# Transposing eight of twelve row blocks by DMA instead of on TensorE, and moving up the last value block's work in the paired feed-forward parts

## The chip, the cores and the metric

The kernel runs on one core of a Trainium2 chip. A core has five engines that run side by side, each through its own list of instructions in order: TensorE (PE) multiplies matrices and can transpose a 128x128 tile by multiplying it with an identity, VectorE (DVE) and ScalarE (ACT) work on tiles in on-chip memory, GpSimd (POOL) and SyncE (SP) here mostly issue transfers (DMAs). Semaphores make one engine wait for another. The metric is device time in microseconds (us) of one execution; the kernel before takes 1997.59 us, the median of three runs (1996.73 to 1998.44).

## The reference

One decoder layer for 256 tokens with 2048 features, all in 32-bit floats:

```python
hn = rmsnorm(h, norm_mix_w)
q, k, v, g_ret, xr, yr, g_a, g_b = jnp.split(hn @ w_in, offsets, axis=-1)
ret_out = silu(g_ret) * head_groupnorm(chunkwise_retention(rotary(q), rotary(k), v))
rnn_out = gelu(yr) * rg_lru(causal_dwconv(xr), ...)
merged = sigmoid(g_a) * (ret_out @ w_proj_ret) + sigmoid(g_b) * (rnn_out @ w_proj_rnn)
h = h + merged @ w_mix_out
h = h + memory_cross_attention(rmsnorm(h), rmsnorm(mem), xa_w_q, xa_w_k, xa_w_v, xa_w_o)
up = causal_dwconv(rmsnorm(h) @ ffn_w_up)          # 2 x 5632 columns: gate, value
gate, val = jnp.split(up, 2, axis=-1)
h = h + (silu(gate) * val) @ ffn_w_down
out = rmsnorm(h, final_norm_w)
```

The sigmoid is written with a tanh, so `merged` is formed at twice its value and has to be scaled by 0.5.

## The kernel before

**How a product is made.** The weights come as tiles of 4 x 128 rows by 512 columns (1 MB, `raw`). ACT rounds a tile to the format that TensorE multiplies at full speed (`hi`, line 286), DVE subtracts to get what was lost (`lo`, line 287). The activations are split in the same way into two halves of one tile (`s`, lines 552 to 557 and 578, 579). A product needs three matmuls: high part of the activation with `hi` (line 362), low part with `hi` (363), both called uppers here, and high part with `lo` (369), the lowers. Four k steps by two row halves make a unit of 24 matmuls for one weight tile.

**Units and pairs.** `gemm_n` computes one block of 512 output columns in four units, one per weight tile. `pair_out` and `pair_add` (both through `pair_products`) compute two neighbouring blocks in eleven units with fewer multiplications, as in Strassen's scheme. Units p0 to p3 take rows of the activations; q1 to q7 take pieces of them or sums of pieces (`ss`, made by `sums`, lines 501 to 510), and need sums of weight tiles: DVE adds two held tiles after q5 (line 294, tile A plus B) and after q6 (line 292, tile A plus C), and a POOL DMA adds a tile from memory into a held one (line 267). A held tile can be changed only once `hi` and `lo` are made from it.

**Order of work.** `units` steps through the plan of all units. Before a unit's matmuls it prepares weight tiles up to two units ahead (`prefetch`). `later(n, fn)` puts a function off until n more units have passed; small steps (transposes, splits, reloads) are placed so between the units. The framework schedules what the code emits once, when the kernel is built, and fixes the order on each engine; `tc.high_priority(URGENT)` moves work ahead of other work that is ready. There are six buffers for `raw` and three for `hi` and `lo`. SP issues weight loads, row loads and stores, and transposing DMAs, in order.

**Turning rows.** A product leaves its result with tokens as rows; the next product needs features as rows. In three places PE turns them: `transposed` (line 532) does four 128x128 transposes into one piece of 256 features; each block of 512 columns has two pieces. `turn_merged` turns the four blocks of `merged` during w_proj_rnn; `turn` and `turn_rows` turn the residual rows `hrow` after w_mix_out and after xa_w_o: twelve blocks in all, 24 groups of four transposes, 96 transposes. The residual of w_mix_out is made as a pair of blocks 0 and 1, then blocks 2 and 3 singly; that of xa_w_o as two pairs.

In other places DMAs turn the rows: `row_planes` copies the 32-bit words of a block into two planes of 16-bit halves (ACT, two copies, line 757), `turn_planes` transposes them with two DMAs on SP (line 1205 before), and `join_planes` puts one piece together again (ACT, two copies, line 763). So the feed-forward's up product (`up`) and the attention's keys work.

**Beside it.** In `residual`, `squares` sums the squares of each finished block for the norm (ACT, line 1113). During w_mix_out, `memory_rows` also loads a block of the memory's rows (line 208) and sums its squares. The residual is stored for later (`hkept`, line 1139).

**Feed-forward.** It runs in parts of 4, 4 and 3 blocks. In a part of four the down product works in pairs. Each up block is turned by DMA, scaled (line 1271), convolved (`conv`: ACT line 1281, DVE line 1283), and gated (`hidden`: lines 1354 to 1356, 555, 556). For the last value block of a paired part, the two joins are put off by 2 and 4 units into the down product's first pair.

Of the kernel before, what the change touches and what calls it, by code (L numbers as in the profile page):

```python
# [9 lines left out]
F32 = mybir.dt.float32  # L10
F32R = mybir.dt.float32r
I32 = mybir.dt.int32
U16 = mybir.dt.uint16
AF = mybir.ActivationFunctionType
ALU = mybir.AluOpType
AX = mybir.AxisListType

P = 128
D = 2048
S = 256  # L20
# [6 lines left out]
FF = 5632  # L27
# [127 lines left out]
def hybrid_layer(  # L155
# [34 lines left out]
    def big(shape, dt=F32, s="b"):  # L190
        return bp.tile(shape, dt, tag="big", name=nm(s))

    def tmp(s="t"):
        return tp.tile([P, 2, S], F32, tag="tmp", name=nm(s))
# [109 lines left out]
    def later(n, fn):  # L304

        pending.append((step[0] + n + 1, fn))
# [187 lines left out]
    def sums(src, scale=None):  # L494

        t = big([P, 2, BW], F32R, s="ss")
        m = tmp("sm")
        f = m.rearrange("p a n -> p (a n)")
        s1, s2, s3, s4 = (f[:, i * P : (i + 1) * P] for i in range(4))
        a11, a21, a12, a22 = (src[:, j, i * P : (i + 1) * P] for j in range(2) for i in range(2))  # L500
        dve.tensor_tensor(out=s1, in0=a21, in1=a22, op=ALU.subtract)
        dve.tensor_tensor(out=s2, in0=s1, in1=a11, op=ALU.subtract)
        dve.tensor_tensor(out=s3, in0=a11, in1=a21, op=ALU.subtract)
        dve.tensor_tensor(out=s4, in0=a12, in1=s2, op=ALU.add)
        if scale is None:
            act.copy(t[:, 0, :], f)
            dve.tensor_tensor(out=t[:, 1, :], in0=f, in1=t[:, 0, :].bitcast(F32), op=ALU.subtract)
        else:
            act.mul(t[:, 0, :], f, scale)
            dve.scalar_tensor_tensor(  # L510
                out=t[:, 1, :], in0=f, scalar=scale, in1=t[:, 0, :].bitcast(F32), op0=ALU.mult, op1=ALU.subtract
            )
        return t
# [34 lines left out]
    def split_pair(src, scale=None):  # L548

        t = big([P, 2, BW], F32R, s="s")  # L550
        if scale is None:
            act.copy(t[:, :, 0:S], src)
            dve.tensor_tensor(out=t[:, :, S:BW], in0=src, in1=t[:, :, 0:S].bitcast(F32), op=ALU.subtract)
        else:
            act.mul(t[:, :, 0:S], src, scale)
            dve.scalar_tensor_tensor(  # L556
                out=t[:, :, S:BW], in0=src, scalar=scale, in1=t[:, :, 0:S].bitcast(F32),
                op0=ALU.mult, op1=ALU.subtract,
            )
        return t  # L560
# [13 lines left out]
    def split_cols(src, wcol):  # L574

        t = big([P, 2, BW], F32R, s="s")
        for j in range(2):
            act.activation(t[:, j, 0:S], src[:, j, :], AF.Identity, scale=wcol(j))
            dve.scalar_tensor_tensor(
                out=t[:, j, S:BW], in0=src[:, j, :], scalar=wcol(j), in1=t[:, j, 0:S].bitcast(F32),  # L580
                op0=ALU.mult, op1=ALU.subtract,
            )
        return t
# [170 lines left out]
    def planes(t, rows, cs=slice(0, BW)):  # L754

        for i in range(2):
            act.copy(t[:, :, i, cs], words(rows)[:, :, :, 1 - i])

    def join_planes(d, pr):

        t = tmp("jp")
        for i in range(2):
            ins = act.copy(words(t)[:, :, :, 1 - i], d[:, i, 2 * pr : 2 * pr + 2, :])  # L763
            if i == 0:
                tc.keep_in_program_order(ins)
        return t

    class KeptRows(list):
        def __init__(self, name, wcol=None):
            self.rows = dp.tile([4, S, 2 * BW], U16, name=name)  # L770
# [244 lines left out]

    def turn_merged(m, pr):
        for t in transposed(m[:, :, pr * S : (pr + 1) * S]):
            if len(merged) < KC:
                c = tmp("mt")
                act.mul(c, t, 0.5)  # L1020
                merged.append(split_pair(c))
                merged_sums.append(sums(c))
            else:
                merged.append(split_pair(t, 0.5))

    for b in range(4):
        recurrent(b)
# [36 lines left out]
    for b in range(4):  # L1064
        m = sig[4 + b]
        gated(m, gemm_n("w_proj_rnn", 0, rnn, NT, b * BW))
        dve.tensor_add(m, m, sig[b])
        for pr in range(2):
            later(pr, lambda m=m, pr=pr: turn_merged(m, pr))


    hrow = [load_rows(x, c) for c in range(2)]
# [2 lines left out]
    def residual(w, st, ssum, out, osum, wcol, steps=None):  # L1075

        ss = sp_.tile([P, 2, 4], F32, tag="ss0", name=nm("ss"))
        for bs in RESIDUAL[w]:
            if steps:
                steps(bs[0])  # L1080
            if len(bs) > 1:
                pair_add(w, 0, st, ssum, bs[0] * BW, bs[1] * BW, hrow[bs[0]], hrow[bs[1]])
            else:
                h = hrow[bs[0]]
                dve.tensor_add(h, h, gemm_n(w, 0, st, NT, bs[0] * BW))
            for i, b in enumerate(bs):
                squares(hrow[b], ss, b)
                for pr in range(2):
                    later(i if bs[0] and len(bs) > 1 else 2 * i + pr, lambda b=b, pr=pr: turn(b, pr, out, osum, wcol))
        return ss  # L1090

    def turn(b, pr, out, osum, wcol):
        with tc.high_priority(URGENT):
            turn_rows(hrow[b][:, :, pr * S : (pr + 1) * S], 4 * b + 2 * pr, out, osum, wcol)
# [22 lines left out]
        dve.tensor_reduce(out=var, in_=ss, axis=AX.X, op=ALU.add)  # L1117
        return rsqrt_small(var, 2, 1.0 / D, EPS)

    rsms = []  # L1120
    ssm = sp_.tile([P, 2, 4], F32, tag="ss0", name="ssm")

    def memory_rows(c):
# [9 lines left out]
                later(1 + 4 * (c - 2), lambda c=c: hrow.append(load_rows(x, c)))  # L1133

    h1s, h1s_sums = [], []
    ss1 = residual("w_mix_out", merged, merged_sums, h1s, h1s_sums, p_xa, memory_steps)
    hkept = dp.tile([4, P, 2, BW], F32, name="hkept")
    for b in range(4):
        sp.dma_start(out=hkept[b], in_=hrow[b])


    lscale = sp_.tile([P, 2], F32, tag="ls", name="lscale")
# [39 lines left out]

    qs = KeptRows("qs")

    def row_planes(o):

        t = big([P, 2, 2, BW], U16, s="rp")
        planes(t, o)
        return t

    for b in (0, 2):
        for i in range(KC):
            if b == 0 and i < 2:
# [3 lines left out]
                later(9 + i // 2, lambda i=i: ms[KC + i])  # L1197
        for i, o in enumerate(pair_out("xa_w_q", h1s, h1s_sums, b * BW)):
            later(1 + 2 * i, lambda b=b + i, o=o: qs.store(b, row_planes(o)))

    def turn_planes(rows):

        d = big([P, 2, KC, S], U16, s="d")
        for tt in range(2):
            sp.dma_start_transpose(
                out=d.rearrange("p a c s -> p (a c) s")[:, :, tt * P : (tt + 1) * P],
                in_=rows[:, tt].rearrange("p a w -> p (a w)"),
            )
        return d

    def turn_key(b, o):
        d = turn_planes(row_planes(o))
# [48 lines left out]
    def up(c0, b, at, then):  # L1261

        if at is None:
            for pr, a in enumerate(gemm_t("ffn_w_up", 0, h2s, NT, c0 + b * BW)):
                then(pr, scaled(a, "uz"))
            return
        d = turn_planes(row_planes(gemm_n("ffn_w_up", 0, h2s, NT, c0 + b * BW)))

        def turned(pr):
            z = join_planes(d, pr)  # L1270
            dve.tensor_tensor(out=z, in0=z, in1=rsb2, op=ALU.mult)
            then(pr, z)

        for pr in range(2):
            later(at[pr], lambda pr=pr: turned(pr))
# [87 lines left out]
    for part, nb_ in enumerate(FF_PARTS):  # L1363
        final = part == len(FF_PARTS) - 1
        paired = nb_ == 4
        hid, hid_sums = [], []
        for b in range(b0, b0 + nb_):
            gt, vl = big([P, 4, S], s="fg"), big([P, 4, S], s="fv")
            last = b + 1 == b0 + nb_
            up(0, b, (1, 2), lambda pr, z, b=b, gt=gt: conv(0, b, pr, z, gt))  # L1370
            if last:
                later(0, lambda part=part, n=2 if paired else 4: get_rows(part % 2, range(n)))

            def finish_up(pr, z, b=b, gt=gt, vl=vl, paired=paired):
                conv(FF, b, pr, z, vl)
                hidden(gt, vl, pr, paired)

            up(FF, b, None if last and not paired else (2, 4) if last else (1, 2), finish_up)
        if final:
            wfin = []  # L1380
            for i in range(2):
                t = big([P, 2, BW], s="wf")
                sp.dma_start(
                    out=t.rearrange("p a n -> p (a n)"),
                    in_=final_norm_w[i * 1024 : (i + 1) * 1024].partition_broadcast(P),
                )
                wfin.append(t)
        if nb_ == 4:
            for b in (0, 2):
                if b == 0:  # L1390
                    later(8, lambda part=part: get_rows(part % 2, (2, 3)))
                pair_add("ffn_w_down", b0 * BW, hid, hid_sums, b * BW, (b + 1) * BW, hrow[b], hrow[b + 1])
                put_rows((part + 1) % 2, (b, b + 1))
        else:
            for b in range(4):
                down(b0, hid, b, final)
        b0 += nb_
# [35 lines left out]
```

## Time and profile before

| | |
|---|---|
| median of three runs | 1997.59 us |
| the profiled execution | 1995.6 us, span 1993.8 us, mean granted clock 0.995 |
| PE busy | 1968.6 us, 9304 matmuls |
| DVE busy | 1566.4 us |
| ACT busy | 1277.2 us |
| POOL busy | 43.2 us |
| data moved | 456.59 MB, 229 GB/s |

The profile is of one execution. Its span runs from the first to the last instruction recorded; the execution's own time is 1.8 us longer. Busy is time in which the engine executes something; a group's row gives the line, engine, operation, tiles, count, busy time, mean duration and the idle time of the engine just before, with what ended it. `SPq` and `POOLq` are the issuing queues. Matmuls overlap, so a matmul that is listed with 0.39 us is followed by the next after 0.227 us; starts are what counts.

### The profile page before, as it was taken

To read this page: it belongs to the slowest core of one execution; us is meant where nothing else is said; L and a number is where in the kernel's file an instruction comes from. 1 tells how busy PE (TensorE), PEld (TensorE's weight loads), DVE (VectorE), ACT (ScalarE), POOL (GpSimd) and SP (SyncE) were. 2 spreads that over 40 slices of the span, in tenths; PEclk is the share of its full clock that TensorE was granted. 3 is DMA by queue.
4 is the path that set the end of the run, shared out by engine and by line. 5 is a ranking of instruction groups with operands and counts; after the bars stand their busy time and mean duration, and the time that the engine had idled before them with its cause. 6 is when DMAs were issued, how large, how long until landed. Compare 5 with 4: busy or idle time off the path is not lost.

```text
span 1993.8 us, 23634 instructions
## 1 busy us (share of the span) xinstructions
PE 1968.6 (99%) x9304; PEld 1650.8 (83%) x9304; DVE 1566.4 (79%) x1546; ACT 1277.2 (64%) x1323; POOL 43.2 (2%) x52
## 2 busy tenths in 40 slices
PE   9999999999999999999999999999989999899998
PEld 7888888888888888888888888888878888788887
DVE  6978888889886886779988778677786777885775
ACT  6655656767677554567778756567744667546662
POOL 0000000000000000000000000000000000000000
PEclk9999999999999999999999999999999999899999
DMA  9675674655887865878998748766777677686671
GB/s 369 233 261 147 223 264 161 230 190 160 266 260 220 248 250 190 252 256 258 270 259 235 267 125 271 236 226 204 234 232 273 207 219 236 204 278 228 211 245 61
DMA packets 146463, 456.59 MB, mean 229 GB/s; under 512 B 77744, under 2 KB 82480, under 8 KB 98608
## 3 DMA queue, kind: packets, MB, share of 16 engines
q1 hardware_dynamic: 139072, 410.51, 58.7%
q0 software_dynamic: 5760, 41.95, 11.6%
q10 hardware_dynamic: 1520, 2.63, 0.4%
q8 instruction: 73, 1.20, 0.2%
q14 instruction: 38, 0.31, 0.0%
HBM read 420.96 MB, written 16.78 MB: 220 GB/s over the span
## 4 chain that ended last, share of the span: by engine, by line
PE 91%; DVE 4%; ACT 2%; DMA 1%; issue 1%; SPq 0%; POOLq 0%; ACTq 0%; DVEq 0%
PE acc L362 25%; PE acc L363 25%; PE acc L369 24%; PE acc L351 14%; PE sm L518 2%; DVE lo L287 1%; ACT hi L286 1%; DMA raw<-in_wall 1%; PE acc L518 1%; PE sm L948 1%; PE sm L532 1%; DVE raw L294 0%; DVE fv L1283 0%; DMA d<-rp 0%; DVE tb L722 0%
## 5 line engine op out<-in xcount | busy, mean ns | idle before, releaser
L287 DVE TENSOR_TENSOR lo<-raw,hi 128x2048 fp32r<-128x2048 f32 (+1 forms) x420 | 950.9, 2267 | 297.8 <-ACT hi L286 297.0
L286 ACT CAST hi<-raw 128x2048 fp32r<-128x2048 f32 (+1 forms) x418 | 793.2, 1901 | 522.7 <-PE acc L363 374.8
L362 PE MATMUL acc<-hi,s 128*128 128x512 f32 x2008 | 787.3, 392 | 12.4 <-ACT hi L286 12.3
L363 PE MATMUL acc<-hi,s 128*128 128x512 f32 x2008 | 784.3, 391 | 0.0
L369 PE MATMUL acc<-lo,s 128*128 128x512 f32 x2008 | 501.1, 389 | 0.0
L362 PEld LDWEIGHTS acc<-hi,s 128*128 128x128 f32 x2008 | 378.6, 189 | 91.5 <-ACT hi L286 13.2
L363 PEld LDWEIGHTS acc<-hi,s 128*128 128x128 f32 x2008 | 378.9, 189 | 78.5 <-DVE s L556 1.0
L369 PEld LDWEIGHTS acc<-lo,s 128*128 128x128 f32 x2008 | 377.1, 188 | 78.3
L351 PE MATMUL acc<-s,hi 128*128 128x512 f32 x832 | 200.4, 392 | 2.1 <-DVE hi L284 1.5
L351 PEld LDWEIGHTS acc<-s,hi 128*128 128x128 f32 x832 | 153.5, 188 | 32.8 <-issue 1.6
L362 PE MATMUL acc<-hi,ss 128*128 128x512 f32 x320 | 125.8, 393 | 0.8 <-ACT o L454 0.6
L363 PE MATMUL acc<-hi,ss 128*128 128x512 f32 x320 | 124.7, 390 | 0.0
L763 ACT COPY jp<-d 128x512 uint16<-128x512 uint16 x132 | 93.4, 771 | 29.4 <-DMA d<-rp 29.3
L351 PEld LDWEIGHTS acc<-s,lo 128*128 128x128 f32 x832 | 107.1, 191 | 4.9 <-DVE lo L287 1.3
L351 PE MATMUL acc<-s,lo 128*128 128x256 f32 x832 | 110.5, 284 | 0.5 <-DVE lo L287 0.5
L369 PE MATMUL acc<-lo,ss 128*128 128x512 f32 x320 | 85.6, 389 | 0.0
L362 PEld LDWEIGHTS acc<-hi,ss 128*128 128x128 f32 x320 | 60.1, 188 | 14.5 <-ACT o L454 1.4
L369 PEld LDWEIGHTS acc<-lo,ss 128*128 128x128 f32 x320 | 60.1, 188 | 12.6
L363 PEld LDWEIGHTS acc<-hi,ss 128*128 128x128 f32 x320 | 60.1, 188 | 12.2
L267 POOL DMA_DIRECT2D raw<-in_wall x40 | 35.2, 880 | 1550.7 <-DVE lo L287 887.5
L427 DVE TENSOR_TENSOR nat<-nat,acc 128x512 f32<-128x512 f32 (+1 forms) x49 | 44.0, 910 | 14.9 <-PE acc L369 14.9
L292 DVE TENSOR_TENSOR raw<-raw,raw 128x2048 f32<-128x2048 f32 x20 | 45.8, 2288 | 0.4
(235 smaller groups left out, 1251.7 us busy)
## 6 DMA issues: line engine op xcount, KB each, us to landing
raw<-in_wall SPq DMA_DIRECT2D x333, 1024.0 KB, 5.0
raw<-in_wall POOLq DMA_DIRECT2D x40, 1024.0 KB, 8.2
fkept<-nat SPq DMA_DIRECT2D x12, 512.0 KB, 7.7
nat<-fkept SPq DMA_DIRECT2D x12, 512.0 KB, 5.6
xt<-in_x_t SPq DMA_DIRECT2D x11, 256.0 KB, 7.8
raw<-in_wall SPq DMA_DIRECT2D x5, 512.0 KB, 7.9
nat<-in_x ACTq DMA_DIRECT2D x4, 512.0 KB, 10.1
ret<-hr SPq DMA_DIRECT2D x4, 512.0 KB, 4.6
```

Of the source, the lines that this page charges most:

```text
L267: pool.dma_start(out=raw, in_=src, accum_op=ALU.add)
L286: act.copy(hi[:, a:b], raw[:, a:b])
L287: dve.tensor_tensor(out=lo[:, a:b], in0=raw[:, a:b], in1=hi[:, a:b].bitcast(F32), op=ALU.subtract)
L292: dve.tensor_tensor(out=to, in0=to, in1=by, op=ALU.add)
L351: pe.matmul(a, part, sx, start=k == 0 and t == 0, stop=k == nk - 1 and t == 0, skip_group_check=True)
L362: pe.matmul(o, h, hi, start=start and kk == 0, stop=False, skip_group_check=True)
L363: pe.matmul(o, l, hi, start=False, stop=False, skip_group_check=True)
L369: pe.matmul(o, h, lo, start=False, stop=stop and kk == KC - 1, skip_group_check=True)
L427: dve.tensor_tensor(out=o, in0=o, in1=i, op=op)
L518: ins = pe.matmul(o, a, b, start=start and i == 0, stop=stop and i == 2, skip_group_check=True)
L532: ins = pe.transpose(t[:, j, tt * P : (tt + 1) * P], rows[:, tt, k + j * P : k + (j + 1) * P], ident)
L763: ins = act.copy(words(t)[:, :, :, 1 - i], d[:, i, 2 * pr : 2 * pr + 2, :])
```

## The change

Eight of the twelve blocks are turned by planes, transposing DMAs and joins: merged blocks 0, 1 and 2 (`turn_merged_by_dma`), residual blocks 0, 1 and 2 of w_mix_out and 0 and 1 of xa_w_o (`turn_by_dma`). The planes and the DMAs are put off by 0 to 2 units (the figures stand in the diff), the joins by a few units more. The other four keep PE's transposes. The factor 0.5 on merged pieces moves into the split and the sums. The stores of residual blocks 0 to 2 are issued right after each block's transposing DMAs. In the feed-forward, the last value block of a paired part has its joins put off by 2 and 2 units instead of 2 and 4, with high priority for all its steps.

```diff
--- before.py
+++ after.py
@@ -765,6 +765,22 @@
                 tc.keep_in_program_order(ins)
         return t
 
+    def row_planes(o):
+
+        t = big([P, 2, 2, BW], U16, s="rp")
+        planes(t, o)
+        return t
+
+    def turn_planes(rows):
+
+        d = big([P, 2, KC, S], U16, s="d")
+        for tt in range(2):
+            sp.dma_start_transpose(
+                out=d.rearrange("p a c s -> p (a c) s")[:, :, tt * P : (tt + 1) * P],
+                in_=rows[:, tt].rearrange("p a w -> p (a w)"),
+            )
+        return d
+
     class KeptRows(list):
         def __init__(self, name, wcol=None):
             self.rows = dp.tile([4, S, 2 * BW], U16, name=name)
@@ -1015,13 +1031,19 @@
 
     def turn_merged(m, pr):
         for t in transposed(m[:, :, pr * S : (pr + 1) * S]):
-            if len(merged) < KC:
-                c = tmp("mt")
-                act.mul(c, t, 0.5)
-                merged.append(split_pair(c))
-                merged_sums.append(sums(c))
-            else:
-                merged.append(split_pair(t, 0.5))
+            merged.append(split_pair(t, 0.5))
+
+    def turn_merged_by_dma(m, n):
+        d = turn_planes(row_planes(m))
+
+        def join(pr):
+            t = join_planes(d, pr)
+            merged.append(split_pair(t, 0.5))
+            if len(merged) <= KC:
+                merged_sums.append(sums(t, 0.5))
+
+        for pr in range(2):
+            later(n + pr, lambda pr=pr: join(pr))
 
     for b in range(4):
         recurrent(b)
@@ -1065,8 +1087,11 @@
         m = sig[4 + b]
         gated(m, gemm_n("w_proj_rnn", 0, rnn, NT, b * BW))
         dve.tensor_add(m, m, sig[b])
-        for pr in range(2):
-            later(pr, lambda m=m, pr=pr: turn_merged(m, pr))
+        if b < 3:
+            later(0, lambda m=m, n=2 if b < 2 else 1: turn_merged_by_dma(m, n))
+        else:
+            for pr in range(2):
+                later(pr, lambda m=m, pr=pr: turn_merged(m, pr))
 
 
     hrow = [load_rows(x, c) for c in range(2)]
@@ -1085,9 +1110,32 @@
                 dve.tensor_add(h, h, gemm_n(w, 0, st, NT, bs[0] * BW))
             for i, b in enumerate(bs):
                 squares(hrow[b], ss, b)
-                for pr in range(2):
-                    later(i if bs[0] and len(bs) > 1 else 2 * i + pr, lambda b=b, pr=pr: turn(b, pr, out, osum, wcol))
+                if b < 2 or b == 2 and len(bs) == 1:
+                    n, m = ((0, 3), (4, 7))[i] if len(RESIDUAL[w]) == 2 else ((0, 2) if b < 2 else (0, 1), (2, 4))[i]
+                    later(n, lambda b=b, m=m - n: turn_by_dma(b, m, out, osum, wcol))
+                else:
+                    for pr in range(2):
+                        later(i if len(bs) > 1 else pr, lambda b=b, pr=pr: turn(b, pr, out, osum, wcol))
         return ss
+
+    def turn_by_dma(b, m, out, osum, wcol):
+        d = turn_planes(row_planes(hrow[b]))
+        if b < len(keep):
+            keep[b]()
+
+        def join(pr):
+            t = join_planes(d, pr)
+            i = 4 * b + 2 * pr
+            if osum is not None and len(out) < KC:
+                for j in range(2):
+                    act.activation(t[:, j, :], t[:, j, :], AF.Identity, scale=wcol(i + j))
+                out.append(split_pair(t))
+                osum.append(sums(t))
+            else:
+                out.append(split_cols(t, lambda j: wcol(i + j)))
+
+        for pr in range(2):
+            later(m + pr, lambda pr=pr: join(pr))
 
     def turn(b, pr, out, osum, wcol):
         with tc.high_priority(URGENT):
@@ -1117,7 +1165,7 @@
         dve.tensor_reduce(out=var, in_=ss, axis=AX.X, op=ALU.add)
         return rsqrt_small(var, 2, 1.0 / D, EPS)
 
-    rsms = []
+    rsms, keep = [], []
     ssm = sp_.tile([P, 2, 4], F32, tag="ss0", name="ssm")
 
     def memory_rows(c):
@@ -1133,10 +1181,11 @@
                 later(1 + 4 * (c - 2), lambda c=c: hrow.append(load_rows(x, c)))
 
     h1s, h1s_sums = [], []
+    hkept = dp.tile([4, P, 2, BW], F32, name="hkept")
+    keep += [lambda b=b: sp.dma_start(out=hkept[b], in_=hrow[b]) for b in range(3)]
     ss1 = residual("w_mix_out", merged, merged_sums, h1s, h1s_sums, p_xa, memory_steps)
-    hkept = dp.tile([4, P, 2, BW], F32, name="hkept")
-    for b in range(4):
-        sp.dma_start(out=hkept[b], in_=hrow[b])
+    sp.dma_start(out=hkept[3], in_=hrow[3])
+    keep.clear()
 
 
     lscale = sp_.tile([P, 2], F32, tag="ls", name="lscale")
@@ -1182,12 +1231,6 @@
 
     qs = KeptRows("qs")
 
-    def row_planes(o):
-
-        t = big([P, 2, 2, BW], U16, s="rp")
-        planes(t, o)
-        return t
-
     for b in (0, 2):
         for i in range(KC):
             if b == 0 and i < 2:
@@ -1197,16 +1240,6 @@
                 later(9 + i // 2, lambda i=i: ms[KC + i])
         for i, o in enumerate(pair_out("xa_w_q", h1s, h1s_sums, b * BW)):
             later(1 + 2 * i, lambda b=b + i, o=o: qs.store(b, row_planes(o)))
-
-    def turn_planes(rows):
-
-        d = big([P, 2, KC, S], U16, s="d")
-        for tt in range(2):
-            sp.dma_start_transpose(
-                out=d.rearrange("p a c s -> p (a c) s")[:, :, tt * P : (tt + 1) * P],
-                in_=rows[:, tt].rearrange("p a w -> p (a w)"),
-            )
-        return d
 
     def turn_key(b, o):
         d = turn_planes(row_planes(o))
@@ -1267,8 +1300,9 @@
         d = turn_planes(row_planes(gemm_n("ffn_w_up", 0, h2s, NT, c0 + b * BW)))
 
         def turned(pr):
-            z = join_planes(d, pr)
-            dve.tensor_tensor(out=z, in0=z, in1=rsb2, op=ALU.mult)
+            with tc.high_priority(URGENT if at[0] == at[1] else 0):
+                z = join_planes(d, pr)
+                dve.tensor_tensor(out=z, in0=z, in1=rsb2, op=ALU.mult)
             then(pr, z)
 
         for pr in range(2):
@@ -1375,7 +1409,14 @@
                 conv(FF, b, pr, z, vl)
                 hidden(gt, vl, pr, paired)
 
-            up(FF, b, None if last and not paired else (2, 4) if last else (1, 2), finish_up)
+            def finish_last(pr, z, finish_up=finish_up):
+                with tc.high_priority(URGENT):
+                    finish_up(pr, z)
+
+            if last and paired:
+                up(FF, b, (2, 2), finish_last)
+            else:
+                up(FF, b, None if last else (1, 2), finish_up)
         if final:
             wfin = []
             for i in range(2):
```

## The prediction

> **What bounds the kernel now.** First the page: engine totals, the chain that ended last, the costliest groups; then what TensorE (PE) waited for.
>
> ```profile
> PE 1968.6 (99%) x9304; PEld 1650.8 (83%) x9304; DVE 1566.4 (79%) x1546; ACT 1277.2 (64%) x1323; POOL 43.2 (2%) x52
> PE 91%; DVE 4%; ACT 2%; DMA 1%; issue 1%; SPq 0%; POOLq 0%; ACTq 0%; DVEq 0%
> ```
> ```profile
> PE acc L362 <- ACT hi L286: 12.3, 2, 6.3
> PE acc L351 <- DVE hi L284: 1.5, 1, 1.5
> ```
>
> PE is busy for 99% of the span and 91% of the chain. A microsecond of PE work removed is gained unless what replaces it comes late. PE has only two waits worth naming, 12.3 us together, both for a weight's high part (hi) from ACT.
>
> **The change part by part.** *1. Sixteen groups of four PE transposes go* (64 of the 96 at L532), two groups per block: merged blocks 0 to 2 six, w_mix_out residual blocks 0 to 2 six, xa_w_o residual blocks 0 and 1 four. The chain, as start, duration and work, shows the price; the shape view shows the count.
>
> ```profile
> 849.62 1.81 PE acc L369 x8
> 855.06 1.82 PE acc L369 x8
> 856.88 0.44 PE sm L532 x4
> 860.99 1.82 PE acc L369 x8
> ```
> ```profile
> L532 PE MATMUL sm<-cid,nat x64: 269/272/273, 856.7 to 1268.1; 128*128 128x128 f32 x64
> L532 PE MATMUL sm<-cid,o x16: 270/272/273, 746.6 to 775.6; 128*128 128x128 f32 x16
> L532 PE MATMUL sm<-cid,sig x16: 270/272/300, 792.1 to 818.5; 128*128 128x128 f32 x16
> ```
>
> A unit of 24 matmuls takes 855.06 − 849.62 = 5.44 us, with a group 860.99 − 855.06 = 5.93. So 0.49 us a group, 16 × 0.49 = 7.8 us off PE.
>
> *2. What replaces them.* Per block: two plane copies on ACT, two transposing DMAs on SP, four join copies on ACT (and two scalings in place of two, for summed pieces). Rows of the same work, ns as min/median/max:
>
> ```profile
> L757 ACT COPY rp<-o x16: 1036/1046/1083, 943.8 to 1091.7; 128x1024 uint16<-128x1024 uint16 x16
> L763 ACT COPY jp<-d x132: 755/769/812, 577.2 to 1911.4; 128x512 uint16<-128x512 uint16 x132
> L791 ACT ACTIVATE jp<-jp,pb x16: 493/507/520, 590.2 to 651.0; 128x256 f32<-128x256 f32 x16
> L552 ACT CAST s<-jp x24: 603/620/643, 591.6 to 1118.9; 128x512 fp32r<-128x512 f32 x24
> L506 ACT CAST ss<-sm x24: 609/620/634, 66.5 to 1152.8; 128x512 fp32r<-128x512 f32 x24
> L578 ACT ACTIVATE s<-sm,pb x24: 454/473/477, 883.8 to 1270.8; 128x256 fp32r<-128x256 f32 x24
> L286 ACT CAST hi<-raw x418: 1046/1913/1947, 8.7 to 1966.5; 128x2048 fp32r<-128x2048 f32 x138, 128x1024 fp32r<-128x1024 f32 x2
> L287 DVE TENSOR_TENSOR lo<-raw,hi x420: 691/2287/2295, 5.8 to 1969.4; 128x2048 fp32r<-128x2048 f32 x137, 128x1024 fp32r<-128x1024 f32 x2, 128x512 fp32r<-128x512 f32 x1
> L1205 SPq DMA_TRANSPOSE d<-rp x50: 1231/1317/4240, 1028.8 to 1900.8; - x50
> DMA to landing us min/median/max: 3.1/3.4/6.6
> ```
>
> A block costs ACT 2 × 1.05 + 4 × 0.77 = 5.2 us, 42 us in all. By stage (windows: length, then busy time of PE, its weight loads, DVE, ACT and POOL, clock, DMA share) that weighs differently:
>
> ```profile
> 786.00:829.00 43.00, 43.00 (x198) 35.38 (x197) 29.72 (x19) 19.86 (x17) 1.73 (x2) 1.00 0.72 223
> 851.45:900.60 49.15, 49.15 (x230) 40.60 (x230) 34.20 (x44) 32.12 (x54) 1.61 (x2) 1.00 0.77 259
> 1212.95:1255.70 42.75, 42.75 (x198) 35.37 (x197) 38.09 (x28) 26.77 (x28) 0.88 (x1) 1.00 0.81 260
> ```
>
> In w_proj_rnn (first row) and xa_w_o (third) ACT goes from 20 to 36 of 43 us and from 27 to 37 of 41: idle time covers it, and following the joins by hand, the last merged pieces are ready some 3 us, the xa_w_o pieces over 8 us before PE asks. Cost zero; if that cover fails, each microsecond it lacks reaches PE. In the single w_mix_out blocks 2 and 3 (second row), ACT would do 32.1 + 6 × 1.05 + 12 × 0.77 + 8 × (0.51 − 0.42) = 48.4 us in 49.15 − 6 × 0.49 = 46.2. It is over-full. Each engine's order is fixed when the kernel is built, so I follow the changed order by hand, with t = 0 where pair (0, 1) ends (851.45).
>
> Block 2 runs 0 to 21.8, block 3 to 43.5, then xa_w_q begins. Its q1 wants the fourth residual piece (block 1, second pair) at 45.0 and then p0 the two of block 2. Block 2's row is added by 23.0. ACT's hi of block 3's second unit waits for PE's uppers of the first (21.8 + 16 × 0.227 = 25.4) and ends 27.3; DVE's lo to 29.7, a low part and four sums of 0.28 behind it to 31.5; ACT's L506, which waits for them, to 32.1; only then block 2's planes, to 34.2. SP issues its two transposes and behind them the load of the last memory rows:
>
> ```profile
> 1434.33 2.61 SPq L1205 DMA_TRANSPOSE d<-rp  x2
> 866.15 0.43 SPq L208 DMA_DIRECT2D nat<-in_mem  x1
> 871.90 0.63 ACT L1113 ACTIVATE junk<-nat 128x512 f32<-128x512 f32 x1 [2.52 <-DMA nat<-in_mem]
> ```
>
> Two transposes occupy SP for 2.6 us, the load takes 871.90 − 866.15 = 5.75: it lands at 34.2 + 2.6 + 5.75 = 42.5, and ACT, in order, stands on its squares until then. Behind them: squares 43.8, two joins 45.3, a hi 47.2, two scalings 48.2, the split 48.8, DVE's low part behind a lo 50.2: 5.2 us late. Then a join, a hi that waits for q1, L506, two joins, two L578, a join, a square, two L578: block 2's second pair is complete at 58.2. PE, due past those matmuls at 49.0, is past them at 58.3: **9.3 us** lost. Where the second transpose takes 4.24 us to issue (the maximum above) and lands later, it is 12. I take the middle, 10.6. Bounds: 0 if ACT runs ahead of what I follow, 12 above.
>
> *3. The feed-forward move.* Both long waits sit in the last value block of a paired part. PE, then ACT and POOL, DVE:
>
> ```profile
> 1457.34 0.39 PE L363 MATMUL acc<-hi,s 128*128 128x512 f32 x1
> 1463.79 1.33 PE L362 MATMUL acc<-hi,s 128*128 128x512 f32 x2 [6.07 <-ACT hi L286]
> 1466.23 0.63 PE L363 MATMUL acc<-hi,s 128*128 128x512 f32 x1
> 1467.94 0.55 PE L363 MATMUL acc<-hi,s 128*128 128x512 f32 x1
> 1728.19 1.33 PE L362 MATMUL acc<-hi,s 128*128 128x512 f32 x2 [6.28 <-ACT hi L286]
> 1734.05 0.61 PE L363 MATMUL acc<-hi,s 128*128 128x512 f32 x1
> ```
> ```profile
> 1438.83 0.77 ACT L763 COPY jp<-d 128x512 uint16<-128x512 uint16 x1 [2.71 <-DMA d<-rp]
> 1455.34 1.92 ACT L286 CAST hi<-raw 128x2048 fp32r<-128x2048 f32 x1 [2.38 <-DMA raw<-in_wall]
> 1461.84 1.90 ACT L286 CAST hi<-raw 128x2048 fp32r<-128x2048 f32 x1 [3.59 <-DVE raw L292]
> ```
> ```profile
> 1447.15 0.89 POOL L267 DMA_DIRECT2D raw<-in_wall  x1 [21.87 <-DVE fv L1283]
> ```
> ```profile
> 1444.21 2.28 DVE L294 TENSOR_TENSOR raw<-raw,raw 128x2048 f32<-128x2048 f32 x1
> 1455.41 2.28 DVE L287 TENSOR_TENSOR lo<-raw,hi 128x2048 fp32r<-128x2048 f32 x1
> 1459.47 2.28 DVE L292 TENSOR_TENSOR raw<-raw,raw 128x2048 f32<-128x2048 f32 x1
> ```
>
> The chain: the join's DMA, L294, POOL's adding DMA (1447.15, read at 1455.34), then DVE's convolution, L292, the hi at 1461.84, PE. The front is untouched. The new order puts L292 ahead of that convolution, behind a lo (now about 1453.6), two products and a split of 0.6 us each: it starts at 1457.6 instead of 1459.5. So the hi, and PE, come 1.9 us earlier, twice: 3.8 us. Bounds: 0 where something else holds L292, and 12.3 where the waits go altogether. I take 3.8 since the adding DMA stays.
>
> *4. The clock.* After each wait matmuls start 0.43 us apart instead of 0.227, until 1468 and 1734: 11 and 16 of them, so 2.5 and 3.5 us. I expect such a tail, 3 us, after the new wait too, and that the two old ones keep theirs (the nearest row, 6.07 us idle, has one).
>
> The Trainium skill, "TensorE: Matmul & The Clock Gate", section "Part 1: The HAM clock gate (the "warmup" mystery)", has the clock halve after an idle window of about 3.4 us and return after a busy one; the windows run freely. By that rule, which the tails above agree with, an idle time cut to about 4.2 us would often miss a whole window and leave no tail.
>
> *5. The rest.* Stores of residual blocks 0 to 2 move up on SP, three issues ahead of weight loads that have units in hand; scaling of the merged sums moves from a copy into L506 and L507: zero.
>
> **The sum.** −7.8 − 3.8 + 10.6 + 3.0 = +2.0. The profiled run took 1995.6 us (span 1993.8), 2.0 below the median of 1997.6, and goes to 1997.6; a median goes to **1999.6**. Its own range: −11.6 + 9.3 + 2.5 to −11.6 + 12 + 3.5, so 1997.8 to 2001.5. Under 0.2% (4 us) a measurement tells little from no change.
>
> **Rivals.** *The new chain is covered:* ACT's slack of 36% holds, xa_w_q starts on time. For it: the run before has no wait there. Against: the over-full window. 1997.6 − 11.6 = 1986.0.
>
> *The feed-forward tails go:* the waits shrink to 4.2 us and the clock stays full: 6.0 less, 1993.6. For it: nothing shows where the tail begins; against: both rows known have it.
>
> *Slower: transposes land late everywhere.* If pairs land near 6.6 us after issue rather than 3.4, behind megabyte loads, the merged pieces' 3 us of cover are used up as well, and w_mix_out's pair stalls by some 2 us, with a tail of 3: 2001.5 + 3 to 5, say 2005. It decides once landings exceed some 6 us in w_proj_rnn, where the DMA share is 0.72.
>
> *The move does nothing:* the waits stay 6 us: 1999.6 + 3.8 = 2003.4.
>
> **How the numbers follow.** As worked 0.38; covered 0.18; tails gone 0.14; late landings 0.20; move without effect 0.10. Tails gone lies on the 0.2% bound, mostly counted as faster. Faster 0.31, same 0.39, slower 0.30. The range leaves out the outer parts of the first and fourth cases: 1986 to 2006.
>
> **What would show it.** Right: 32 transposes left at L532; a PE wait for split pieces (s, lines 552 to 579) of some 5 us and two or three shorter ones at the start of xa_w_q, with ACT's squares waiting for nat<-in_mem just before; PE's two hi waits near 4.2 us. Wrong: no wait in xa_w_q, or hi waits gone or as long as before, or waits for merged pieces in w_mix_out.

## The result, and the profile after

The changed kernel is slower. Over nine runs each, its median is 2005.09 us (1997.0 to 2020.4) against 1996.73 us (1995.07 to 1998.62); the ratio is 1.0047, 95% interval 1.0029 to 1.0064. Its runs lie 23 us apart, those of the kernel before less than 4, and its fastest is as fast as they are: a part of the loss is in some runs only. The profiled run took 2000.3 us, with a span of 1998.5; it is not one of the long ones.

First the run that was profiled. From its page, busy time and the chain; then what TensorE waited for, and what is left at L532.

```profile
PE 1966.8 (98%) x9240; PEld 1646.4 (82%) x9240; DVE 1566.6 (78%) x1546; ACT 1309.8 (66%) x1367; POOL 43.2 (2%) x52
PE 84%; DVE 5%; ACT 4%; DMA 3%; issue 3%; SPq 1%; POOLq 0%; ACTq 0%; DVEq 0%
```
```profile
PE acc L362 <- ACT hi L286: 7.3, 3, 3.5
PE acc L362 <- ACT s L552: 4.7, 1, 4.7
PE acc L362 <- ACT s L578: 1.6, 1, 1.6
PE acc L363 <- DVE s L556: 1.6, 2, 0.9
PE acc L363 <- DVE s L553: 1.5, 1, 1.5
...
PE acc L362 <- ACT o L456: 1.1, 1, 1.1
...
PE sm L605 <- DVE s L579: 0.9, 1, 0.9
```
```profile
L532 PE MATMUL sm<-cid,nat x24: 271/273/421, 902.9 to 1275.2; 128*128 128x128 f32 x24
L532 PE MATMUL sm<-cid,sig x8: 271/272/327, 810.8 to 815.1; 128*128 128x128 f32 x8
```

PE has 64 matmuls fewer. Its two long waits for a hi are shorter (6.1 and 6.3 us before, 3.2 and 3.5 now), and there are new waits for split pieces (`s`). The same matmuls of both traces, set side by side by their start, give the loss by place:

| place | matmul before | after | lead of the changed kernel, so far |
|---|---|---|---|
| end of w_proj_rnn | 799.3 | 796.1 | 3.3 us ahead |
| start of w_mix_out | 835.9 | 833.4 | 2.5 ahead |
| last single block of w_mix_out | 887.7 | 882.3 | 5.4 ahead |
| xa_w_q, after its first units | 904.5 | 911.1 | 6.6 behind |
| xa_w_k | 1043.8 | 1051.7 | 7.9 behind |
| xa_w_o, second pair | 1230.9 | 1237.1 | 6.1 behind |
| first up block | 1273.5 | 1281.5 | 8.0 behind |
| after the first feed-forward wait | 1465.8 | 1471.8 | 6.0 behind |
| last compared | 1985.3 | 1990.0 | 4.7 behind |

Two traces can differ by up to 1.4 us at 799.3, before any change that they contain (as that of the xa_w_o blocks alone does, further down), so only the larger steps count. In four later traces of the same kernel 12.5 to 13.6 us go at the start of xa_w_q; the steps that the prediction put at zero (w_mix_out's pair, xa_w_k, the first up block) are 4.0 us together here and 0.4 to 2.3 there.

So 12 us go at the start of xa_w_q. PE there, with the wait before each row in brackets; then ACT, with SP's issues behind it:

```profile
893.45 0.39 PE L363 MATMUL acc<-hi,s 128*128 128x512 f32 x1
898.56 0.59 PE L362 MATMUL acc<-hi,s 128*128 128x512 f32 x1 [4.73 <-ACT s L552]
900.64 0.80 PE L363 MATMUL acc<-hi,s 128*128 128x512 f32 x1 [1.49 <-DVE s L553]
905.60 1.22 PE L362 MATMUL acc<-hi,s 128*128 128x512 f32 x2 [1.60 <-ACT s L578]
```
```profile
883.47 1.99 ACT L757 COPY rp<-nat 128x1024 uint16<-128x1024 uint16 x2
892.69 0.63 ACT L1161 ACTIVATE junk<-nat 128x512 f32<-128x512 f32 x1 [1.76 <-DMA nat<-in_mem]
895.16 1.89 ACT L286 CAST hi<-raw 128x2048 fp32r<-128x2048 f32 x1
897.89 0.62 ACT L552 CAST s<-jp 128x512 fp32r<-128x512 f32 x1
```
```profile
885.49 2.88 SPq L778 DMA_TRANSPOSE d<-rp  x2
888.42 0.57 SPq L208 DMA_DIRECT2D nat<-in_mem  x1
```

This is the chain of the prediction: block 2's planes, two transposes, the memory rows' load behind them, ACT on the squares, and the join, hi, scaling and split only then. The wait for L552 measured 4.73 us. But ACT was not over-full: from the pair's end (849.0) to PE's wait it was busy for 34.5 of 44.6 us, and of the rest it stood 6.0 us on memory rows, 4.3 of them on the block of rows before the last. So the work would have fitted; what made it late is where, in its order, it had to wait.

**What only some runs have.** A second profile of the same kernel happened to be of a run of about 2009 us (span 2007.7). Up to xa_w_o it agrees with the first within 2 us; there it loses 9 us more. First what PE, then what ACT waited for in that run; then SP and POOL there (start, issue time); last, of the two transposes of that block and of POOL's DMA behind them, the time to landing.

```profile
PE acc L362 <- DVE nat L427: 9.5, 2, 9.0
```
```profile
ACT jp L763 <- DMA d<-rp: 11.6, 2, 11.2
```
```profile
1234.64 3.68 SPq L778 DMA_TRANSPOSE d<-rp  x2
```
```profile
1236.59 0.88 POOL L267 DMA_DIRECT2D raw<-in_wall  x1 [17.79 <-ACT jp L763]
```
```profile
DMA to landing us min/median/max: 4.6/10.9/17.3
```
```profile
raw<-in_wall POOLq DMA_DIRECT2D x1, 1024.0 KB, 18.8
```

The same two views of the first profile:

```profile
DMA to landing us min/median/max: 5.0/6.9/8.7
```
```profile
raw<-in_wall POOLq DMA_DIRECT2D x1, 1024.0 KB, 10.3
```

The second of these transposes, of xa_w_o's block 1, landed after 17.3 us (8.7 in the first profile), and POOL's adding DMA, issued 0.66 us behind it, after 18.8 (10.3). ACT, in order, stood at the join, DVE then waited 8.4 us for ACT's split, and PE for DVE. What the DMA engines did in those nine microseconds, in slices, for the long run and for the same nine of the first profile:

```profile
GB/s 53 83 49 89 1 36 0 38 0 0 38 0 0 38 0 0 38 0 0 38 0 1 18 73 36 38 73 0 38 36 0 38 73 0 38 182 0 110 0 1
DMA packets 115, 0.28 MB, mean 31 GB/s; under 512 B 83, under 2 KB 83, under 8 KB 83
```
```profile
DMA packets 341, 2.14 MB, mean 237 GB/s; under 512 B 81, under 2 KB 81, under 8 KB 81
```

In the long run hardly anything moved. The packet records show the adding DMA's 8 KB packets taking up to 10.2 us each, against 0.63 us as a rule, while 162 packets of the transposes were still to come when the first of them began; in the first profile it was 102 packets, and the longest took 2.1 us.

### The profile page after: what moved, and what is told of

The parts are those of the page before. It is cut to its first block, busy times and chain, and to the rows that moved or that the text cites. A ratio compares the mean times of both kernels' runs of the same rounds, so it can differ in the third digit from the quotient of the medians.

```text
span 1998.5 us, 23574 instructions
## 1 busy us (share of the span) xinstructions
PE 1966.8 (98%) x9240; PEld 1646.4 (82%) x9240; DVE 1566.6 (78%) x1546; ACT 1309.8 (66%) x1367; POOL 43.2 (2%) x52
## 4 chain that ended last, share of the span: by engine, by line
PE 84%; DVE 5%; ACT 4%; DMA 3%; issue 3%; SPq 1%; POOLq 0%; ACTq 0%; DVEq 0%
PE acc L362 23%; PE acc L363 23%; PE acc L369 22%; PE acc L351 13%; DVE lo L287 2%; ACT hi L286 2%; PE sm L518 2%; DMA raw<-in_wall 1%; DMA nat<-in_mem 1%; PE acc L518 1%; DMA d<-rp 1%; PE sm L964 1%; SPq L778 1%; ACT jp L763 0%; ACT junk L1161 0%
## 5 line engine op out<-in xcount | busy, mean ns | idle before, releaser
L763 ACT COPY jp<-d 128x512 uint16<-128x512 uint16 x164 | 116.7, 770 | 39.5 <-DMA d<-rp 38.1
L363 PEld LDWEIGHTS acc<-hi,ss 128*128 128x128 f32 x320 | 60.7, 190 | 12.5
L369 PEld LDWEIGHTS acc<-lo,ss 128*128 128x128 f32 x320 | 60.1, 188 | 12.6
L427 DVE TENSOR_TENSOR nat<-nat,acc 128x512 f32<-128x512 f32 (+1 forms) x49 | 44.0, 909 | 12.3 <-PE acc L369 10.6
```

The costliest lines, as they stand in the source:

```text
L363: pe.matmul(o, l, hi, start=False, stop=False, skip_group_check=True)
L369: pe.matmul(o, h, lo, start=False, stop=stop and kk == KC - 1, skip_group_check=True)
L427: dve.tensor_tensor(out=o, in0=o, in1=i, op=op)
```

## The experiments

**Each part alone.** My theory had one costly part, the w_mix_out residual; a rival looked for the spread of the runs in each of the others.

*Feed-forward move alone* (all blocks turned on PE):

```diff
-            up(FF, b, None if last and not paired else (2, 4) if last else (1, 2), finish_up)
+            if last and paired:
+                up(FF, b, (2, 2), finish_last)
+            else:
+                up(FF, b, None if last else (1, 2), finish_up)
```

> Only the feed-forward part of the change. My theory: both hi waits of PE shrink by about 1.9 us each and nothing else moves, so 3.5 to 4.5 us faster than before (about 0.998 of it), and the runs lie as close together as those of before (within 4 us). Rival (the spread of the changed kernel's runs, 1997 to 2020 us, comes from the feed-forward waits, whose length now lies where the clock sometimes drops): the runs spread by 10 us or more.

Measured: 1993.48 us (1991.48 to 1997.24), ratio 0.9986 (0.9977 to 0.9996), 2.8 us faster by the ratio; the traces stand 4.1 us apart. That is a little less than expected, and the runs lie 5.8 us apart instead of 4; the rival's 10 us are not there.

*Merged blocks 0 to 2 alone:*

```diff
+        if b < 3:
+            later(0, lambda m=m, n=2 if b < 2 else 1: turn_merged_by_dma(m, n))
```

> Only the merged blocks 0 to 2 are turned by DMA. My theory: six groups of transposes gone, 2.9 us, less some 0.8 us for one short hi wait in w_mix_out's pair: 2 to 3 us faster, runs close together. Rival (late landings of transposes use up the 3 us of cover in some runs): no gain in the median and runs that spread by 10 us.

Measured: 1999.3 us (1996.35 to 2001.67), ratio 1.0007 (0.9998 to 1.0017): no gain, against the theory, and without the rival's spread. The six groups are gained (2.4 us at the end of w_proj_rnn) and given back far away, in xa_w_k (4.2 us up to its end) and in the second paired part of the feed-forward, where every engine's order is that of the kernel before. There a weight load, two transposes and ACT's wait, before and in this kernel, each with the landing of POOL's adding DMA ahead of them (issued at 1688.56 and 1690.73):

```profile
raw<-in_wall POOLq DMA_DIRECT2D x1, 1024.0 KB, 7.9
```
```profile
1695.16 0.33 SPq L265 DMA_DIRECT2D raw<-in_wall  x1
1698.52 2.95 SPq L1205 DMA_TRANSPOSE d<-rp  x2
```
```profile
1703.38 0.77 ACT L763 COPY jp<-d 128x512 uint16<-128x512 uint16 x1 [3.06 <-DMA d<-rp]
```
```profile
raw<-in_wall POOLq DMA_DIRECT2D x1, 1024.0 KB, 10.4
```
```profile
1698.33 0.33 SPq L265 DMA_DIRECT2D raw<-in_wall  x1
1700.69 4.96 SPq L778 DMA_TRANSPOSE d<-rp  x2
```
```profile
1709.29 0.77 ACT L763 COPY jp<-d 128x512 uint16<-128x512 uint16 x1 [6.81 <-DMA d<-rp]
```

The transposes follow the load after 2.4 us instead of 3.4. The load lands after 7.5 us instead of 4.8, the transposes after 6.2 and 7.2 instead of 3.7 and 3.5, and PE loses 3.6 us. The closeness does not do it: in the first profile of the changed kernel the transposes follow the load after 2.7 us at this place (1702.53 and 1705.19) and land after 3.3. What does go with it is the adding DMA. Over all 18 traces, here and at the same place in the first paired part, the two transposes landed after 4.8 to 7.2 us in the six cases in which POOL's DMA ahead of them took 9.3 us or more, and after 3.1 to 3.8 us in the thirty in which it took less. Which of them holds up which, no run separates; nor was it shown that the median run has this.

*w_mix_out's residual blocks 0 to 2 alone:*

```diff
+                if b in ((0, 1, 2) if w == "w_mix_out" else ()):
...
+                    later(n, lambda b=b, m=m - n: turn_by_dma(b, m, out, osum, wcol))
```

> Only the residual blocks 0 to 2 of w_mix_out are turned by DMA, with their stores moved up. My theory: this part alone makes the changed kernel slower: three us gained, 12 to 15 lost at the start of xa_w_q, one more in xa_w_k: 9 to 13 us slower than before, and the spread of the runs is here too. Rival (the loss needs the merged blocks' earlier finish as well, or comes from elsewhere): within 4 us of before.

Measured: 2008.73 us in four runs (2005.64 to 2009.19), ratio 1.0057 (1.0042 to 1.0072), 11.4 us slower. PE's wait for L552 is there (3.4 us) with those behind it; 11.2 us go between 887.7 and 904.5. So this part alone makes the loss at xa_w_q. In its trace 5.0 us more go in the feed-forward, which it leaves as before; in the second paired part the transposes land late there as in merged alone. The four runs lie close together, against the expectation; four are few to say that the spread is not from here.

*xa_w_o's residual blocks 0 and 1 alone:*

```diff
+                if b in (() if w == "w_mix_out" else (0, 1)):
...
+                    later(n, lambda b=b, m=m - n: turn_by_dma(b, m, out, osum, wcol))
```

> Only the residual blocks 0 and 1 of xa_w_o are turned by DMA. My theory: two us gained from four groups, and as much lost again in short waits at the start of the feed-forward part (0.9 us at line 605 and 0.5 us before it in the changed kernel's trace): within 2 us of before, runs close together. Rival (the spread comes from here): runs 10 us apart.

Measured: 1999.85 us (1998.47 to 2002.01), ratio 1.0016 (1.0006 to 1.0025): 3 us slower, just outside what I expected, and close together. The 0.9 us wait at L605 is there, and in the trace xa_w_o comes out even (1.8 us gained, 1.9 lost), as the theory had it; 2.3 us go in the feed-forward. POOL's adding DMA follows the second transpose after 0.7 us here too, and none of the ten runs is long; in the trace only 7 packets of the transposes are left when its own begin.

**Taking one thing out of the changed kernel.** The changed kernel again, on the same chip as the next three:

> The changed kernel once more, beside the others. My theory: 3 to 9 us slower than before; its trace shows again some 11 us lost at the start of xa_w_q. If its runs spread over 10 us again, the trace should show where: landings of transposes near 7 us instead of 3.5 (theory: transposes issued on top of a fresh weight load), against longer idle times of the same waits with a half clock behind them (rival).

Measured: 1999.91 us (1998.17 to 2019.31), ratio 1.0034 (1.0009 to 1.0059): six of ten runs below 2000, four from 2005 to 2019. Its trace is the long run shown above: 12.6 us go at xa_w_q, and the landing that makes it long takes 17.3 us, not 7.

*The last memory rows six units later:*

```diff
-                later(5 + 4 * c, lambda c=c: memory_rows(c))
+                later(5 + 4 * c + (6 if c == 3 else 0), lambda c=c: memory_rows(c))
```

> The changed kernel with the last memory rows loaded and squared six units later, in xa_w_q, so that ACT no longer stands on that load ahead of the joins of w_mix_out. My theory (ACT's order carries the wait at xa_w_q): the fourth piece is split by 44 instead of 50 us after the pair, in time; some 2 to 3 us remain at p0; 8 to 10 us faster than the changed kernel, 1 to 5 us faster than before. Rival (the joins are late because ACT has too much work, or because transposes land late): at most 4 us faster than the changed kernel.

Measured: 2002.38 us (1993.56 to 2012.97), ratio 1.0015 (0.9995 to 1.0036). The wait for L552 is down to 0.3 us in the trace, but 7.0 us go at xa_w_q instead of 2 to 3. ACT's order does carry that wait, and I undercounted what is left: DVE's low parts and the two pieces of block 2 come late as well (waits of 1.0, 1.9 and 0.4 us). ACT still stands on the block of memory rows before, 4.6 us where it was 2.5 in the kernel before, and is busy for 25.8 of the 27.1 us from there to xa_w_q:

```profile
867.09 0.64 ACT L1161 ACTIVATE junk<-nat 128x512 f32<-128x512 f32 x1 [4.62 <-DMA nat<-in_mem]
```

Whether these 4.6 us make the 7.0 was not tried. The median is no faster than the changed kernel's, against the theory, and says nothing more, because this kernel has long runs too: in its trace the same transpose in xa_w_o lands after 16.6 us and PE waits 8.3.

*Block 2 of w_mix_out back on PE:*

```diff
-                if b < 2 or b == 2 and len(bs) == 1:
+                if b in ((0, 1) if w == "w_mix_out" else (0, 1)):
...
-                        later(i if len(bs) > 1 else pr, lambda b=b, pr=pr: turn(b, pr, out, osum, wcol))
+                        later(i if bs[0] and len(bs) > 1 else 2 * i + pr + 2 * (b == 2), lambda b=b, pr=pr: turn(b, pr, out, osum, wcol))
```

> The changed kernel with block 2 of the w_mix_out residual back on PE's transposes, two units later than before. My theory: without block 2's planes and the two transposes ahead of the memory rows' load, that load comes some 4 us earlier, the fourth piece is in time and p0 loses 2 to 3 us; one microsecond for two groups of PE transposes comes back: 7 to 9 us faster than the changed kernel. Rival (the loss is of blocks 0 and 1): as slow as the changed kernel.

Measured: 1993.45 us (1989.62 to 1996.25), ratio 0.9975 (0.9965 to 0.9985). That is 0.9975 / 1.0034, 0.6% or 12 us faster than the changed kernel beside it, more than expected, because there were no long runs either; the medians are 6.5 us apart. The mechanism was not as expected: between 887.7 and 904.5 it still loses 8.2 us, not 2 to 3, so most of that loss is of blocks 0 and 1, as the rival had it. That the long runs went as well, with xa_w_o's code untouched, was not foreseen; in its trace the two transposes there land after 3.2 us, and none of their packets is left when those of POOL's DMA begin.

*All of w_mix_out back on PE:*

> The changed kernel with all of w_mix_out's residual back on PE's transposes; merged and xa_w_o blocks still by DMA, feed-forward moved. My theory: no wait at the start of xa_w_q; the sum of the three other parts as they were timed alone, -3 for the feed-forward, +1 for merged and +3 for xa_w_o, gives 0 to 2 us slower than before; by my steps it would be 6 to 8 us faster. If the parts alone were slow only through the feed-forward's old waits, which transposes now landed on worse, it comes out nearer the second.

Measured: 1992.17 us (1987.97 to 2003.47), ratio 0.9975 (0.9957 to 0.9992), 5 us faster than before: a little short of what my steps gave, and better than the parts alone add up to. Nothing is lost at the start of xa_w_q in its trace. One of its eight runs took 2003.5 us.

*xa_w_o's block 1 moved in time,* first earlier, then later:

```diff
-                    n, m = ((0, 3), (4, 7))[i] if len(RESIDUAL[w]) == 2 else ...
+                    n, m = ((0, 3), (2, 7))[i] if len(RESIDUAL[w]) == 2 else ...     # earlier
+                    n, m = ((0, 3), (5, 8))[i] if len(RESIDUAL[w]) == 2 else ...     # later
```

> The changed kernel with the planes and transposes of xa_w_o's block 1 put off by 2 units instead of 4, which moves them 1 to 2 us earlier and so out of the way of POOL's adding DMA that follows. My new theory (the long runs come from that one place, where transposes still in flight when the adding DMA begins hold both up for about 9 us): no run above 2002 us, median 1997 to 2000. Rival (the long runs come from several places, or from the clock): as before, some runs at 2005 to 2020.

> The changed kernel with those planes and transposes put off by 5 units instead of 4, so that they are issued while the adding DMA moves its data. New theory in its strong form (any such overlap stalls both): nearly every run 8 us or more above 1998. Weak form (only some overlaps do, when transposes were there first): no more long runs than the changed kernel has. The later joins alone may cost 1 to 3 us at the start of the feed-forward part.

Measured: earlier 1999.51 us (1995.29 to 2009.48), ratio 1.0014 (1.0 to 1.0027), with nine of ten runs below 2004 and one at 2009.5, so the median is as expected, but three runs are above 2002, where the theory allowed none; later 2002.14 us (1998.87 to 2005.27), ratio 1.0023 (1.0013 to 1.0032). SP and POOL in the earlier one, then in the later one:

```profile
1229.92 5.34 SPq L778 DMA_TRANSPOSE d<-rp  x2
```
```profile
1233.68 0.87 POOL L267 DMA_DIRECT2D raw<-in_wall  x1 [17.78 <-DVE raw L294]
```
```profile
1248.37 5.18 SPq L778 DMA_TRANSPOSE d<-rp  x2
```
```profile
1241.82 0.87 POOL L267 DMA_DIRECT2D raw<-in_wall  x1 [23.12 <-DVE raw L294]
```

The earlier kernel has 3.8 and 2.5 us between the transposes and POOL's DMA, and 33 packets left when its own begin; the second transpose still landed after 10.2 us, POOL's DMA after 9.5. The later one was meant to force the overlap and did the opposite: its transposes waited on SP behind a weight load until POOL's DMA had nearly landed, 6.5 us after its issue. So it doesn't test the strong form; it is a second kernel without the overlap, and its longest run took 2005.3 us. These two and the next kernel ran on another chip than the changed kernel, which was not run there.

*Both repairs, memory rows later and block 1 earlier:*

> Both repairs: the memory rows later, and xa_w_o's block 1 earlier. My theory (these two places are the whole loss): my own sum with 3 us left at xa_w_q, one in xa_w_k and two at the feed-forward's start, -7.8 - 4 + 6, so 5 to 6 us faster than before, 1990 to 1993 us, no run above 1998. Rival: no faster than the changed kernel's best run, 1997.

Measured: 1994.42 us (1991.46 to 1997.97), ratio 0.9983 (0.9974 to 0.9992). No run is above 1998, as expected; the gain is 3.4 us rather than 5 to 6, since xa_w_q still loses 6.9.

**A faster kernel.** *Feed-forward move and merged blocks 0 and 1 only:*

```diff
+        if b in (0, 1):
+            later(0, lambda m=m, n=2 if b < 2 else 1: turn_merged_by_dma(m, n))
```

> Only the feed-forward move and the merged blocks 0 and 1 by DMA, all else as before; a candidate for the fastest. Four groups gone, 2.0 us, and 4 us in the feed-forward, nothing new late: 5 to 6 us faster than before, 1990 to 1992. Rival (each added transpose makes later landings worse, as merged alone was not faster): 3 us faster at most.

Measured: 1991.88 us (1989.38 to 1994.73), ratio 0.9974 (0.9965 to 0.9983), 5.2 us by the ratio and the shortest spread of those that beat the kernel before.

**Four more profiled runs of the changed kernel,** to see whether the longest runs have a second place:

> The changed kernel, one look, for the trace. Theory: if this run is over 2004 us, its trace has a transposing DMA of xa_w_o's block 1 and POOL's adding DMA behind it that both land after 16 us or more, and PE waits 8 to 9 us for it there; at 1997 to 2001 they land within 11. Rival: a long run without that, or with another place.

> The changed kernel, a second look, same expectation. A run near 2014 to 2020 should show two or more such places.

> The changed kernel, a third look, same expectation: over 2004 us with landings of 16 us or more in xa_w_o, or else within 2001 us.

> The changed kernel, a fourth look, same expectation: over 2004 us with landings of 16 us or more in xa_w_o, or else within 2001 us.

Measured: 1998.81, 1998.68, 1997.28 and 1999.01 us, beside one run of the kernel before at 1998.47. None was long; the second transpose landed after 5.9, 8.5, 8.0 and 3.7 us, POOL's DMA within 10.3. The packets of the transposes still to come when POOL's own began were 37 to 89 in these four and 102 in the first profile; in the two traces with the stall they were 162 and, with the memory rows moved, 279. Long runs did not show here, and whether those at 2014 to 2020 us hold two such places stays open. Over all runs, nine of the changed kernel's 23 runs took more than 2005 us; of the 30 of the three kernels with block 1 moved, two did, on a chip on which the changed kernel was not run.

## Why the prediction was wrong

**Transposes off PE, 7.8 us:** right. The leads in the table grow by 3.3, 2.9 and 1.8 us over the three places, 8.0 together.

**The new wait at xa_w_q, 10.6 us and a tail of 3:** right in place and nearly in size, and in cause for a part. 12.0 us were lost, tail included; the wait for L552 was 4.73 us where the steps had 5.2. That ACT stands on the last memory rows' load is shown by the kernel that moves it; that this is only some 5 of the 12 us is what the steps did not see. The sum of 48.4 us of ACT's work in 46.2 pointed at the right place but was not what bound: ACT had 10.1 us of idle time there. What makes the other 7 us is open.

**The feed-forward move, 3.8 us:** right. PE's interval of 6.45 us became one of 1.11 and one of 3.62; two matmuls take 0.45 of that, so 6.2 lost became 4.3, 1.9 less. Alone the part gave 4.1 us in the traces. That the waits would be near 4.2 us was off, since the rest came as a wait of its own ahead of them.

**The tails:** they stayed, as taken. After the shorter wait:

```profile
1465.77 0.50 PE L363 MATMUL acc<-hi,s 128*128 128x512 f32 x1 [0.73 <-DVE s L556]
...
1469.95 0.79 PE L362 MATMUL acc<-hi,s 128*128 128x512 f32 x1 [3.22 <-ACT hi L286]
1470.54 0.63 PE L363 MATMUL acc<-hi,s 128*128 128x512 f32 x1
...
1475.24 0.60 PE L363 MATMUL acc<-hi,ss 128*128 128x512 f32 x1
1475.66 0.41 PE L362 MATMUL acc<-hi,ss 128*128 128x512 f32 x1
```

The rival in which they go has fallen: in all 18 traces these two waits are followed by 6 to 14 matmuls that start some 0.43 us apart. The Trainium skill, "TensorE: Matmul & The Clock Gate", section "Part 1: The HAM clock gate (the "warmup" mystery)", asks for an idle window of about 3.4 us. Here 3.22 us of idle time, a microsecond after another of 0.73, was enough, and in the trace of the kernel with all of w_mix_out back on PE one of 2.37 us was, after which matmuls start 0.42 to 0.46 us apart; the measurement decides.

```profile
1724.58 0.66 PE L363 MATMUL acc<-hi,s 128*128 128x512 f32 x1 [2.37 <-DVE s L556]
1725.04 0.63 PE L362 MATMUL acc<-hi,s 128*128 128x512 f32 x1
1725.46 0.63 PE L363 MATMUL acc<-hi,s 128*128 128x512 f32 x1
```

**Cost zero in w_mix_out, xa_w_k and at the first up block:** too low by some 4 us in the profiled run: 0.8, 1.3 and 1.9 in the table. Among the waits there are short ones for a hi, an output copied late and a split. In the four later traces only the last is left, 0.5 to 2.0 us.

**The step that failed** is "Cost zero" for the joins of xa_w_o, and with it the idea that a transpose lands after 6.6 us at the latest, the maximum before. With the terms above, a run without long landings comes out near the forecast: the spans of the four later traces are 1.7 to 3.4 us above that of the kernel before, the first profile's 4.7, and six of the ten runs were 0.4 to 2.2 us above the median beside them. But the changed kernel, in xa_w_o, puts two transposes some 2 us and 0.7 us ahead of POOL's adding DMA, where the kernel before has no transposing DMA at all, and in one traced run of six (and in the one of the kernel with the memory rows moved) both stand still for nine microseconds: 17.3 us to landing instead of 6.6 at most. The rival "transposes land late" had the kind of thing right, and its place (w_proj_rnn), its size (2 us) and its being the same in each run wrong; that it named 2005 us, the median measured, is luck. Two traces show the stall, and kernels in which fewer transposing packets are left at that place (0 to 33 in their traces) hardly have long runs. That the stall makes the long runs which were not traced is argued: no run of this kernel near the median of 2005 us was traced, and the kernels with block 1 moved ran on another chip. What the DMA engines wait for in it was not shown, and overlap alone does not suffice: in the kernel with block 2 on PE an adding DMA in xa_w_k ran with some 720 transposing packets and landed after 9.0 us.

## What to carry to other kernels

Work taken off a full engine is gained only if its replacement fits into what the other engines do in the same stage. Here the sum of ACT's work in one window pointed at the place, but it was ACT's order, followed step by step, that gave the wait: ACT stood on loads while it had work left to do. A transposing DMA's usual landing time is not a bound: the longest landings here had an accumulating DMA issued beside them, so look for one before relying on it. Judge such a change by many runs, since five of the six single profiles of this one are 2 to 5 us from that of the kernel before and the median of nine is 8.

## What the runs showed of the hardware that was not expected

- A transposing DMA and an adding DMA behind it landed after 17.3 and 18.8 us (16.6 and 18.1 in a second kernel), instead of 3.7 to 8.7 and 8.9 to 10.3 in five other traces of the changed kernel, with 31 GB/s moved meanwhile.
- In the paired feed-forward parts two transposes landed after 4.8 to 7.2 us where the adding DMA ahead of them took 9.3 to 10.4 us, and after 3.1 to 3.8 where it took 7.8 to 9.2, whether they followed the weight load between after 2.6 or 3.4 us.
- An idle time of 3.22 us on PE was followed by 12 matmuls 0.43 us apart, and one of 2.37 us by matmuls 0.42 to 0.46 us apart.
